# Other SBUF byte offsets for the operands of a decoder block's matmuls, seven weight forms set apart by 32 bytes, and one PSUM bank per product in the feed-forward units

## The chip, the cores and the metric

One Trainium2 chip, one core of it. The metric is device time in microseconds (us): the median of several runs, and beside it the time of one profiled execution, from which all rows of a profile come. The kernel before has a median of 838.19 us over 3 runs (837.63 to 838.41); its profiled execution took 837.62 us.

## The reference

One decoder block in float32 for one sequence of 512 tokens and a model width of 1024:

```python
h = rms_norm(x, norm_mix_pre)
proj = h @ w_in                                  # 1024 -> all q, k, v, gates
o_gla = gla_mixer(...)                           # chunked gated linear attention, 4 heads
o_nsa = nsa_mixer(...)                           # compressed, selected and window attention, 8 heads
mixed = sigmoid(merge_gla) * (o_gla @ w_proj_gla) + sigmoid(merge_nsa) * (o_nsa @ w_proj_nsa)
x = x + rms_norm(mixed @ w_out, norm_mix_post)
h = rms_norm(x, norm_ffn_pre)
f = (silu(h @ w_ffn_gate) * (h @ w_ffn_up)) @ w_ffn_down      # 1024 -> 2816 -> 1024
x = x + rms_norm(f, norm_ffn_post)
```

## The kernel before

**Products in three matmuls.** A float32 operand is split into a high part (a cast to the matmul's reduced float type, `F32R`) and a low part (the rest). A product of weights and activations is three matmuls for each block of 128 inputs: high weights with high activations, high weights with low activations, low weights with high activations (`prod`, L208 to L210, and the same three in the other product helpers). A matmul has a stationary operand, a block of 128 columns of weights, which a weight load brings into TensorE ahead of it, and a moving operand, a strip of 128 to 512 columns of activations. In a row such as `ps_mm<-hT_hi,w_d0h` the moving operand stands first and the stationary one second. Only the token-major products (L318 to L320) have it the other way: tokens stationary, weights moving.

**Seven products for eight.** Most of the input projection (`in_unit`, product at L422), of the feed-forward network (`unit`, L1588) and of its down projection (`down_product`, L1900) goes by a scheme of seven block products: the tokens fall into two halves of 256, the inputs into two halves, and sums and differences of weight blocks (forms a11, s2, s3, s1, a22, s4, a12) meet sums and differences of activation blocks (forms b11, t2, t3, t1, t4, b22, b21). So nearly all matmuls there move 256 columns, in a run of 12 per product (21 in the down projection). A weight pair of 1024 columns holds two forms: a11 and a12, s1 and s2, s3 and s4.

**Stages, in order of time.** Token-major products and the pre-norm; the input projection in 12 units; gated linear attention; sparse attention, with the rest of the input and merge projections woven in (512-column matmuls); the output projection by token halves (256 columns); three plain feed-forward blocks; 19 feed-forward units by seven products, the first two or three of them interleaved with each other; the part of the down projection that is not in the scheme (512 columns); the down projection by seven products; the last norm and the store.

**What sets the order.** The program is written as a sequence in Python; a tile framework puts in the semaphores and the places of tiles, and `tc.issue_after` pins some instructions behind others. Each engine then runs its own list in order. SyncE's queue fetches raw weights; ScalarE (ACT) casts the high parts and writes negated copies of raw weights; GpSimd (POOL) issues the transfers that add the raw weights to those, which makes low parts without VectorE; VectorE (DVE) makes the remaining low parts, the sums and differences of weights, and reads the products out of PSUM. `unit(n)` runs through its seven products in the order a11, s2, s3, s1, a22, s4, a12. After a11, ACT copies the bank piece `r1` into `us` (L1605); DVE adds the later pieces (L1592); at the end ACT applies Silu to `wk` and to `r1` (L1601).

**Where tiles lie in SBUF.** A tile's byte offset in its partition follows from the order and the sizes of the allocations in its pool. Rows of 1024 float32 are multiples of 128 bytes, so a small tile (a vector of constants, a mask) shifts all that lie behind it in a pool by the rest of its size. No line of the kernel before speaks of such offsets. Weights of the streams alternate between two buffers of `whi` and two of `wlo`; others go to `w_d0h`, `w_d0l`, `w_d1h`, `w_d1l`, `w_uu`, `w_rw`, `w_hl`, `w_g3h`, `w_g3l`, `we`, in the input projection to `s0`, `s1`, `s2` and `uu`.

**PSUM.** Eight banks of 512 float32, allocated as four names (`mm`, `acc`, `tp`, `sc`) of two buffers each. A feed-forward unit takes both buffers of one name: `r1` and `rb` share a bank, and so do `r2` and `ra`; the four names take turns over four units. A product that starts in a bank in which another piece is alive must not clear the bank (the argument `first`).

## Time and profile before

| what | value |
|---|---|
| median of 3 runs | 838.19 us (837.63 to 838.41) |
| the profiled execution | 837.62 us |
| its span, first to last instruction | 835.8 us |
| mean granted TensorE clock | 0.999 of full speed |
| TensorE busy | 829.5 us, 5676 matmuls |
| VectorE busy | 655.4 us |
| ScalarE busy | 525.8 us |
| GpSimd busy | 178.4 us |

PE stands for TensorE's matmuls and PEld for its weight loads. Matmuls are pipelined: one starts long before the one ahead of it has ended, and the ends are modelled. So the mean time of one matmul in a group is longer than the distance from its start to the next start; the difference between two groups is what counts.

### The profile page before, as it was taken

The page shows a single profiled execution, that of the slowest core. Times are in us where ns is not written, and L with a number is a line of the kernel's source. Part 1 is how long each engine was busy: PE and PEld are TensorE (multiplying, and loading weights), DVE is VectorE, ACT ScalarE, POOL GpSimd, SP SyncE. Part 2 cuts the span into 40 slices and gives each one's busy share as a digit, 9 for nine tenths or more (in the row PEclk, how much of TensorE's full clock was granted, in tenths as well). Part 3 has the DMA queues.
Part 4 walks back from the last instruction along what each step waited for, and adds up shares of the span by engine and source line. Part 5 has one row for each costly group of instructions (what it writes and reads, how often), then busy time and mean ns, then how long its engine had stood idle before and what let it go on. Part 6 is the DMA issues. An engine that isn't in the chain of part 4 may idle for free.

```text
span 835.8 us, 14964 instructions
## 1 busy us (share of the span) xinstructions
PE 829.5 (99%) x5676; PEld 763.9 (91%) x5676; DVE 655.4 (78%) x1225; ACT 525.8 (63%) x953; POOL 178.4 (21%) x217
## 2 busy tenths in 40 slices
PE   9999999999999999999999999999999999999997
PEld 8999999988888888888878998999999999889996
DVE  7877989956678988877585388998777779739985
ACT  7765687646536878877445588576555667435543
POOL 0223222422321111111001355111111110001444
PEclk9999999999999999999999999999999999999999
DMA  7588788421233444444148759488777772325222
GB/s 256 143 220 185 172 178 184 91 76 50 84 130 92 98 114 121 107 110 105 39 126 327 198 150 235 113 224 205 194 195 184 188 160 65 106 83 177 89 102 102
DMA packets 45449, 120.75 MB, mean 144 GB/s; under 512 B 5981, under 2 KB 11373, under 8 KB 45249
## 3 DMA queue, kind: packets, MB, share of 16 engines
q1 hardware_dynamic: 30720, 82.62, 29.9%
q0 software_dynamic: 14080, 36.76, 24.7%
q8 instruction: 44, 0.72, 0.3%
q10 hardware_dynamic: 576, 0.41, 0.2%
q14 instruction: 29, 0.23, 0.1%
HBM read 105.10 MB, written 4.19 MB: 131 GB/s over the span
## 4 chain that ended last, share of the span: by engine, by line
PE 94%; DVE 3%; ACT 1%; DMA 0%; issue 0%; SPq 0%; DVEq 0%; ACTq 0%
PE ps_mm L208 6%; PE ps_mm L209 6%; PE ps_mm L210 6%; PE ps_mm L1588 6%; PE ps_sc L1588 5%; PE ps_tp L1588 5%; PE ps_acc L1588 5%; PE ps_sc L1900 4%; PE ps_mm L422 4%; PE ps_tp L422 4%; PE ps_acc L422 3%; PE ps_sc L422 3%; PE ps_tp L1137 2%; PE ps_acc L1900 2%; PE ps_mm L1900 2%; PE ps_sc L210 1%
## 5 line engine op out<-in xcount | busy, mean ns | idle before, releaser
L79 ACT CAST whi<-wraw 128x1024 fp32r<-128x1024 f32 (+3 forms) x56 | 54.2, 968 | 50.9 <-issue 13.3
L208 PE MATMUL ps_mm<-hT_hi,whi 128*128 128x512 f32 x152 | 61.8, 407 | 0.0
L86 DVE TENSOR_TENSOR wlo<-wraw,whi 128x1024 fp32r<-128x1024 f32 (+3 forms) x41 | 44.8, 1093 | 20.8 <-ACT whi L79 16.8
L210 PE MATMUL ps_mm<-hT_hi,wlo 128*128 128x512 f32 x152 | 60.0, 395 | 0.0
L209 PE MATMUL ps_mm<-hT_lo,whi 128*128 128x512 f32 x152 | 59.9, 394 | 0.0
L1096 ACT ACTIVATE p<-p,mx 128x512 f32<-128x512 f32 (+1 forms) x64 | 35.8, 559 | 9.2 <-DVE mx L1094 8.4
L226 DVE TENSOR_TENSOR pl<-ps_tp,ph 128x512 fp32r<-128x512 f32 (+1 forms) x64 | 31.2, 489 | 10.2 <-ACT ph L225 9.3
L1094 DVE CUSTOM_DVE_ANT_0 p<-ps_sc,causal 128x512 f32<-128x512 f32 (+1 forms) x64 | 30.0, 485 | 7.4 <-PE ps_sc L1087 7.2
L210 PEld LDWEIGHTS ps_mm<-hT_hi,wlo 128*128 128x128 f32 x152 | 28.6, 188 | 6.4 <-DVE wlo L86 0.3
L1463 POOL DMA_DIRECT2D w_uu<-in_w_up x19 | 16.8, 882 | 81.2 <-PE ps_mm L1588 20.9
L208 PEld LDWEIGHTS ps_mm<-hT_hi,whi 128*128 128x128 f32 x152 | 28.6, 188 | 5.5
L83 POOL DMA_DIRECT2D wlo<-wraw x15 | 13.2, 879 | 94.3 <-ACT wlo L82 93.8
L209 PEld LDWEIGHTS ps_mm<-hT_lo,whi 128*128 128x128 f32 x152 | 28.7, 189 | 4.4
L225 ACT CAST ph<-ps_tp 128x512 fp32r<-128x512 f32 (+1 forms) x64 | 26.4, 414 | 4.4 <-PE ps_tp L1137 3.7
L1137 PE MATMUL ps_tp<-ident,p 128*128 128x128 f32 x160 | 27.7, 272 | 0.0
L1137 PEld LDWEIGHTS ps_tp<-ident,p 128*128 128x128 f32 x160 | 20.8, 140 | 7.1
L208 PE MATMUL ps_mm<-gla_hi,whi 128*128 128x512 f32 x64 | 26.2, 409 | 0.0
L210 PE MATMUL ps_mm<-gla_hi,wlo 128*128 128x512 f32 x64 | 25.2, 394 | 0.0
L209 PE MATMUL ps_mm<-gla_lo,whi 128*128 128x512 f32 x64 | 25.2, 393 | 0.0
L1481 ACT CAST w_d1h<-s 128x1024 fp32r<-128x1024 f32 x13 | 13.6, 1050 | 16.2 <-issue 12.8
L1481 ACT CAST w_d0h<-s 128x1024 fp32r<-128x1024 f32 x12 | 12.6, 1050 | 17.2 <-issue 12.7
L1881 POOL TENSOR_TENSOR y<-y,us 128x256 f32<-128x256 f32 x6 | 6.8, 1155 | 71.8 <-DVE us L1878 71.8
(1270 smaller groups left out, 3436.1 us busy)
## 6 DMA issues: line engine op xcount, KB each, us to landing
wraw<-in_w_t SPq DMA_DIRECT2D x28, 512.0 KB, 3.6
wraw<-in_w_gate SPq DMA_DIRECT2D x21, 512.0 KB, 4.2
rw<-in_w_up SPq DMA_DIRECT2D x19, 512.0 KB, 4.7
wlo<-wraw POOLq DMA_DIRECT2D x15, 512.0 KB, 4.5
wlo<-in_w_gate POOLq DMA_DIRECT2D x13, 512.0 KB, 7.2
urw<-in_w_t SPq DMA_DIRECT2D x12, 512.0 KB, 5.7
w_uu<-in_w_up POOLq DMA_DIRECT2D x19, 256.0 KB, 4.1
raw<-in_w_down SPq DMA_DIRECT2D x10, 448.0 KB, 3.3
```

What stands on the lines that cost most here:

```text
L79: self.cast = self.nc.scalar.copy(hi[:, :cols], raw[:, :cols])
L86: self.nc.vector.tensor_tensor(out=lo[:, :cols], in0=raw[:, :cols], in1=hi[:, :cols].bitcast(F32), op=OP.subtract)
L208: pe.matmul(ps[:, t], wh[:, c], xh(k)[:, t], start=(k == 0), stop=False)
L209: pe.matmul(ps[:, t], wh[:, c], xl(k)[:, t], start=False, stop=False)
L210: marks.append(pe.matmul(ps[:, t], wl[:, c], xh(k)[:, t], start=False, stop=(k == ktot - 1)))
L226: return dve.tensor_tensor(out=lo, in0=src, in1=hi.bitcast(F32), op=OP.subtract)
L422: pe.matmul(o, w[:, c], x_of(b, q, low), start=(first and q == 0 and i == 0), stop=(q == 3 and i == 2), skip_group_check=True)
L1094: dve.tensor_tensor_reduce(out=o, in0=s, in1=causal[:, S - n:S], scale=-1.0, scalar=-NEG, op0=OP.add, op1=OP.min, accum_out=mx[:, i:i + 1])
L1096: act.activation(out=o, in_=o, func=AF.Exp, scale=-1.0, bias=mx[:, i:i + 1], accum_out=z[:, i:i + 1])
L1137: queued["turn"] = pe.transpose(tp[:, i * 128:(i + 1) * 128], p[:, OFF[i] + k * 128:OFF[i] + (k + 1) * 128], ident)
L1588: pe.matmul(o, w[:, c], x[q], start=(first and q == 0 and i == 0), stop=(q == 3 and i == 2), skip_group_check=True)
L1900: pe.matmul(o, w[:, c], x[q], start=(first and q == 0 and i == 0), stop=(q == KH - 1 and i == 2), skip_group_check=True)
```

## The change

**One buffer for the stream weights.** Both pairs of `whi` and `wlo` become views into one tile `wbuf` of 4 x 1024 + 128 columns (class `Regions`). `regions.pair(i, shift)` gives pair 0 or 1, moved by `shift` columns; `SHIFT` is 16 columns (64 bytes), `TURN` 8 columns (32 bytes).

**Offsets.** Constants are packed into one small tile, other small tiles are moved or new (`cst`, `room`, `off2`, `off4`, the 16 spare columns of `hlc`), some allocations change their order (a `room` pass fixes the places of the feed-forward tiles), and `wbuf` is used with `SHIFT` for 256-column products and without it for 512-column ones. The byte offsets modulo 128 of the matmuls' operands become:

| operands | before | after |
|---|---|---|
| `hT_hi`, `hT_lo` (activations; reused for activation forms) | 96 | 96 |
| `t1` to `t4` forms of the input projection | 64 | 96 |
| `h2h`, `h2l`; `x4h`, `x4l`; `x` (b22) in the feed-forward part | 0 | 96 |
| `x5h`, `x5l` | 32 | 96 |
| `gla_hi`, `bh`, `bl`, attention's `q`, `ph`, `pl`, `kas` ... | 0 | 96 |
| stream weights (`whi`, `wlo`, then `wbuf`), 256 columns | 96 | 32 |
| stream weights, 512 columns | 96 | 96 |
| `s1`, `s2` | 96 | 32 |
| `s0` and `uu` of the input projection, `w_g3` | 64 | 32 |
| `w_rw`, `w_hl` | 0 | 32 |
| `w_d0`, `w_d1`, `w_uu` | 32 | 32 |
| `we` | 32 | 96 |
| down projection, high activation forms | 0, 32, 64, 96 | 96, but 32 for one of them |
| down projection, low weights, where the low activations lie at 32 | 64 or 96 | 96 |

**Seven forms set apart.** Seven pairs of weights lie 32 bytes further, at 64 in place of 32: the `a` pairs of input units 0, 5 and 6 (`slot_of`), the gate pairs of feed-forward units N0+3 and N0+9 (`prep_g`), and the down forms 0 and 6 of the sequence (`make`).

**The difference between the two operands.** Take a matmul and the one behind it on TensorE, and the byte offset of the moving operand of the first minus that of the stationary operand of the second, modulo 128. By this the matmuls of reduced float type fall into four groups. Of those with 256 columns:

| difference | before | after |
|---|---|---|
| 0 | 1153 | 115 |
| 32 | 648 | 158 |
| 64 | 951 | 3402 |
| 96 | 923 | 0 |

Of those with 512 columns nearly all but the ones in the stages of the output and the plain feed-forward blocks were at 0 and stay there; after the change 1052 are at 0, 24 at 64 and 3 at 32, and before it about 280 were at 32 or 96. The 158 at 32 are the products of the seven forms and a few at the start of the feed-forward units.

**PSUM.** From unit N0+2 on a feed-forward unit takes two names of two buffers, (`tp`, `sc`) or (`mm`, `acc`) in turn, and each of `r1`, `r2`, `rb`, `ra` has a bank of its own, so that s3 and s1 start their banks; the last unit takes `mm` and `sc`. Units N0 and N0+1 take `tp` and `sc` in the old way.

**Small things.** The mask `triu` is loaded and cast by POOL at the gates in place of DVE later; the mask `keep` is set once in place of twice; the low gate of head 3 and the factors of linear attention have other rooms; the differences of gate 3 are made one unit earlier.

On ACT, at the ends of two of the feed-forward units, before the change (`us` is the copy of the first product, `sl` holds Silu's results, `w_...` are weight parts):

```order
L1601 ACTIVATE sl<-wk 128x256
L1459 CAST whi<-wraw 128x1024
L1601 ACTIVATE sl<-ps_tp 128x256
L1461 ACTIVATE wlo<-wraw 128x1024
L1605 COPY us<-ps_sc 128x256
```

and at the same place after it:

```order
L1636 ACTIVATE sl<-wk 128x256
L1492 CAST wbuf<-wraw 128x1024
L1636 ACTIVATE sl<-ps_tp 128x256
L1494 ACTIVATE wbuf<-wraw 128x1024
L1640 COPY us<-ps_mm 128x256
```

The order is the same; the unit that starts takes the names `mm` and `acc` in place of `sc` alone.

On PE, where the third and fourth feed-forward units (banks `mm` and `acc`) begin inside the first ones, before the change:

```order
L1588 MATMUL ps_sc<-x4l,w_g3h 128x256
L1588 MATMUL ps_sc<-x4h,w_g3l 128x256
L1588 MATMUL ps_mm<-hT_hi,w_d1h 128x256
L1588 MATMUL ps_mm<-hT_lo,w_d1h 128x256
L1588 MATMUL ps_acc<-hT_hi,whi 128x256
L1588 MATMUL ps_acc<-hT_lo,whi 128x256
L1588 MATMUL ps_acc<-hT_hi,wlo 128x256
```

and where units begin inside others after it:

```order
L1623 MATMUL ps_tp<-hT_lo,wbuf 128x256
L1623 MATMUL ps_tp<-hT_hi,wbuf 128x256
L1623 MATMUL ps_mm<-hT_hi,wbuf 128x256
L1623 MATMUL ps_mm<-hT_lo,wbuf 128x256
L1623 MATMUL ps_tp<-x4h,wbuf 128x256
L1623 MATMUL ps_tp<-x4l,wbuf 128x256
L1623 MATMUL ps_sc<-hT_hi,w_hl 128x256
```

The first products of later units stand at other places among those of the first three units; from the sixth unit on the order on PE is the same as before.

The diff, cut to its core:

```diff
+SHIFT = 16
+TURN = 8
+class Regions:
+    def __init__(self, pool, first):
+        self.buf, self.turn = pool.tile([128, 4 * 1024 + 128], F32R, name="wbuf"), first
+    def pair(self, i, shift, cols=1024):
+        at = 2048 * (i % 2) + shift
+        return self.buf[:, at:at + cols], self.buf[:, at + 1024:at + 1024 + cols]
+    def next(self, shift=0):
+        self.turn += 1
+        return self.pair(self.turn - 1, shift)
...
-                hi = self.pool.tile([128, 1024], F32R, tag="whi", bufs=2, name="whi")
-                lo = self.pool.tile([128, 1024], F32R, tag="wlo", bufs=2, name="wlo")
+                hi, lo = self.regions.next(SHIFT if key in self.shifted else 0)
...
     def slot_of(j, what):
         n = 3 * j + (1 if what == "a" else 0 if what == "s1" else 2)
-        return slots[n % 5]
+        at = TURN if (j, what) in ((0, "a"), (5, "a"), (6, "a")) else 0
+        return [x[:, at:at + 1024] for x in slots[n % 5]]
...
-        slots.extend([wts.tile([128, 1024], F32R, tag="w" + x, bufs=2, name="w" + x) for x in ("hi", "lo")]
-                     for _ in range(2))
+        slots.extend((regions.pair(0, SHIFT), regions.pair(1, SHIFT, 1024 + TURN)))
...
-h2h, h2l = quads("h2h", 4, F32R, "hh"), quads("h2l", 4, F32R, "hl")
+h2h, h2l = quads("h2h", 4, F32R, "hh"), quads("h2l", 2, F32R, "hl")
+h2l23 = hlc(F32R, "h2l23")[:, 0:2048].rearrange("p (b a t) -> p b a t", b=2, a=2)
...
     def prep_g(n, after=None):
-        hi, lo = w_slot(("w", "g3", "w")[(n - N0) % 3])
+        hi, lo = w_slot(("w", "g3", "w")[(n - N0) % 3], SHIFT + (TURN if n in (N0 + 3, N0 + 9) else 0))
...
     def unit(n, between=None):
-        tag = ("mm", "acc", "tp", "sc")[(n - N0 + 2) % 4]
-        p1, p2 = bank(tag), bank(tag)
-        r1, rb, r2, ra = p1[:, 0:256], p1[:, 256:512], p2[:, 0:256], p2[:, 256:512]
+        if n < N0 + 2:
+            p1, p2 = [bank(("tp", "sc")[n - N0]) for _ in range(2)]
+            r1, rb, r2, ra = p1[:, 0:256], p1[:, 256:512], p2[:, 0:256], p2[:, 256:512]
+        else:
+            tags = ("mm", "sc") if n == KF - 1 else (("tp", "sc"), ("mm", "acc"))[(n - N0) % 2]
+            r1, r2, rb, ra = [bank(tag)[:, 0:256] for tag in tags for _ in range(2)]
...
-        product(rb, "s3", "t3", False)
+        product(rb, "s3", "t3", n >= N0 + 2)
...
-        product(ra, "s1", "t1", False)
+        product(ra, "s1", "t1", n >= N0 + 2)
...
-        lambda: dform("t3", [quad(x, F32R, "dt3" + x) for x in ("d0h", "d0l", "e0", "e1")], left, h1),
+        lambda: dform("t3", [quad(x, F32R, "dt3" + x) for x in ("e0", "e1", "d0h", "d0l")], left, h1),
...
+    FAR = ("b11", "t2", "t3", "t1")
...
-        hi, lo = [x[:, :KW] for x in w_slot(("w", "g3", "w")[j % 3])]
+        which = ("w", "g3", "w")[j % 3]
+        at = (SHIFT if which == "w" else 0) + (TURN if j in (0, 6) else 0)
+        hi, lo = [x[:, c:c + KW] for x, c in zip(w_slot(which, 0), (at, at + (SHIFT if b in FAR else 0)))]
```

102 lines of the change are left out of this document (58 added, 44 removed).

## The prediction

> **What bounds the kernel now.** I read the page first: the span, the busy times, the chain of work that ended last.
>
> ```profile
> span 835.8 us, 14964 instructions
> PE 829.5 (99%) x5676; PEld 763.9 (91%) x5676; DVE 655.4 (78%) x1225; ACT 525.8 (63%) x953; POOL 178.4 (21%) x217
> PE 94%; DVE 3%; ACT 1%; DMA 0%; issue 0%; SPq 0%; DVEq 0%; ACTq 0%
> ```
>
> PE is busy for 829.5 of 835.8 us. Then the waits of PE alone (line, what it waited for; us in total, times, longest):
>
> ```profile
> PE ps_acc L149 <- DVE eps L136: 0.9, 1, 0.9
> PE ps_sc L1588 <- ACT us L1605: 0.5, 1, 0.5
> PE ps_mm L1588 <- DVE w_hl L1488: 0.4, 1, 0.4
> ```
>
> All waits come to 1.8 us, so only fewer matmuls or a shorter distance between their starts can move the end by more. The change issues the same matmuls. So the question is the distance, and I went from the page to single matmuls. The timeline (start, duration, engine, line, tiles) at both ends of some runs:
>
> ```profile
> 457.60 0.28 PE L208 MATMUL ps_sc<-hT_hi,w_uu 128*128 128x256 f32 x1
> 468.37 0.28 PE L210 MATMUL ps_acc<-hT_hi,we 128*128 128x256 f32 x1
> ...
> 582.78 0.28 PE L1588 MATMUL ps_mm<-hT_hi,whi 128*128 128x256 f32 x1
> 583.50 0.28 PE L1588 MATMUL ps_mm<-hT_hi,w_d0h 128*128 128x256 f32 x1
> 587.62 0.28 PE L1588 MATMUL ps_mm<-hT_hi,w_d0l 128*128 128x256 f32 x1
> ```
>
> From 457.60 to 468.37 lie 95 matmuls of 256 columns: 113.4 ns from start to start. From 582.78 to 583.50 lie 6: 120 ns. From 583.50 to 587.62 lie 35: 117.7 ns. The granted clock is full in all three (the windows below), so it isn't the clock. Groups kept apart by shape show the same by their mean (last number but one, ns), which is the distance and some 163 ns of pipeline:
>
> ```profile
> L208 PE MATMUL ps_mm<-hT_hi,w_d1h 128*128 128x256 f32 x8 | 2.2, 276 | 0.0
> ...
> L209 PE MATMUL ps_mm<-hT_lo,w_d1h 128*128 128x256 f32 x8 | 2.2, 281 | 0.0
> ...
> L1588 PE MATMUL ps_mm<-hT_hi,w_d0h 128*128 128x256 f32 x8 | 2.2, 281 | 0.0
> ...
> L422 PE MATMUL ps_sc<-hT_lo,whi 128*128 128x256 f32 x4 | 1.1, 283 | 0.0
> ...
> L422 PE MATMUL ps_acc<-t2l,s1h 128*128 128x256 f32 x4 | 1.1, 283 | 0.0
> L422 PE MATMUL ps_acc<-t2h,s1h 128*128 128x256 f32 x4 | 1.1, 281 | 0.0
> L422 PE MATMUL ps_acc<-t2h,s1l 128*128 128x256 f32 x4 | 1.1, 279 | 0.0
> ...
> L1395 PE MATMUL ps_sc<-h2h,whi 128*128 128x256 f32 x12 | 3.4, 286 | 0.0
> L1396 PE MATMUL ps_sc<-h2l,whi 128*128 128x256 f32 x12 | 3.3, 279 | 0.0
> ...
> L208 PE MATMUL ps_tp<-hT_hi,whi 128*128 128x512 f32 x32 | 12.4, 389 | 0.0
> ...
> L208 PE MATMUL ps_acc<-h2h,we 128*128 128x512 f32 x8 | 3.2, 396 | 0.0
> ```
>
> The windows are 457.6 to 468.3, 478.3 to 483.6, 583.4 to 587.7, 111.4 to 115, 95 to 98.7, 498.8 to 502.8, 715 to 754 and 511.9 to 520.4. Line, engine and size don't order these rows; the byte offsets of the two operands do, by the difference that the change's second table counts. `hT_hi` (96) with `whi` (96) is difference 0: 283, always 120 ns once it runs. `t2` (64) with `s1` (96) is 96, `h2h` (0) with `whi` (96) is 32: uneven, 118 and 117 to 118 ns on average. `hT_hi` (96) with `w_d1h`, `w_d0h` or `w_uu` (32) is 64: 276 in one place and 281 in two others, for the same tiles. With 512 columns difference 0 takes 389 and 96 takes 396.
>
> So difference 64 has **two rhythms**, 113.4 and 117.7 ns. Inside a run neither changes to the other: the 96 matmuls from 457.60 stay fast, the 46 from 478.2 and the 37 from 583.4 stay slow. What stands ahead of a run seems to choose. After a settled run of difference 0 it is slow in all of 9 cases, of which the first and the last:
>
> ```profile
> L1588 PE MATMUL ps_sc<-hT_hi,w_d1h 128*128 128x256 f32 x4 | 1.1, 281 | 0.0
> ...
> L1588 PE MATMUL ps_mm<-hT_hi,w_d0h 128*128 128x256 f32 x7 | 2.0, 281 | 0.0
> ```
>
> After difference 96 it is either. After fp32 matmuls or a stall it was fast three times and slow once (478.2). After difference 32 it was fast in 4 of 5 cases; the first of those four and the fifth, which follows one single such matmul:
>
> ```profile
> L1588 PE MATMUL ps_tp<-hT_lo,w_d0h 128*128 128x256 f32 x4 | 1.1, 276 | 0.0
> ...
> L1900 PE MATMUL ps_sc<-dt1e,wlo 128*128 128x256 f32 x6 | 1.7, 280 | 0.0
> ```
>
> **The change part by part.** *The long runs.* The change puts 3402 of 3675 matmuls at difference 64, in runs of up to 756, and each of the seven forms set apart is two runs of 11 or 12 (in the down projection one of 20) at difference 32 ahead of a long one. By the cases above such a run starts fast, and I take 113.4 for it. The stages today, by line and window (window, its length, PE busy and matmuls, PEld the same, clock, DMA share, GB/s; the last row is of all instructions, with DVE third, ACT fourth and POOL fifth):
>
> ```profile
> 42.00:167.00 125.00, 120.73 (x1008) 120.33 (x1008) 1.00 0.75 172
> ...
> 554.00:712.00 158.00, 157.03 (x1333) 156.75 (x1332) 1.00 0.71 170
> ...
> 754.00:826.00 72.00, 70.34 (x588) 69.78 (x588) 1.00 0.33 112
> ...
> 520.00:554.00 34.00, 32.96 (x269) 31.96 (x268) 33.45 (x56) 21.65 (x34) 4.23 (x5) 1.00 0.66 160
> ```
>
> Input projection (first row): 120.73 us for 1008, 119.8 ns each; 0.9 of that is what breaks by other matmuls add, which stay, so 118.8. After: 935 at 113.4 and 69 at 117.3, 113.7 on average. Gain 1004 x 5.1 ns = 5.1 us. Feed-forward units (second row): 117.8, without breaks 117.7; after 1289 at 113.4 and 37 at 117 to 120, 113.6. Gain 1326 x 4.1 = 5.4 us. Down projection (third row): 119.6, without the breaks at the norm 118.1; after 543 at 113.4 and 41 at 117.5, 113.7. Gain 584 x 4.3 = 2.5 us.
>
> *Other stages.* Output projection: its present runs are already half at 113.4; 48 go to difference 0 (`w_d1l` to `we`) at 120, and what follows them will be slow: +0.2 us, between 0 and +0.5. Plain blocks: 170 at 64 in place of 0 and 32, cut up by fp32 sums: -0.5, between 0 and -0.7. Attention and plain blocks with 512 columns: some 280 move from 32 or 96 to mostly 0, worth up to 7 ns each (396 against 389), but where attention waits for softmax nothing: -0.7, between 0 and -1.9. Start of the feed-forward units (last row): DVE is busy 33.45 of 34 us, so faster matmuls wait for DVE there; the interleaving moves later products to other places. I take -0.2, between +1.0 (a product that comes before its weights) and -2.0 (PE's whole lost time there, 34 less 269 matmuls at some 118 ns).
>
> *Four banks.* A unit's s3 no longer shares a bank with r1. No wait of PE stood on that, so nothing is gained. The price could be the earlier reuse, two units on in place of four. ACT and PE at the end of one unit:
>
> ```profile
> 621.55 0.41 ACT L1601 ACTIVATE sl<-wk 128x256 f32<-128x256 f32 x1
> 621.95 1.06 ACT L1459 CAST whi<-wraw 128x1024 fp32r<-128x1024 f32 x1
> 622.90 0.38 ACT L1601 ACTIVATE sl<-ps_sc 128x256 f32<-128x256 f32 x1
> ...
> 621.75 0.28 PE L1588 MATMUL ps_sc<-x4h,wlo 128*128 128x256 f32 x1
> 621.86 0.28 PE L1588 MATMUL ps_mm<-hT_hi,w_g3h 128*128 128x256 f32 x1
> ```
>
> The last reader of the bank, Silu, ends at 623.28, 1.4 us into the next unit; the unit that takes the bank again starts a whole unit (some 9.6 us) later. That covers it by 8 us. Only N0+2 takes `sc` straight from N0+1; there s3 comes two products (2.7 us) in, so at worst some 0.5 us once, which the +1.0 above holds. *The rest* (one `triu` cast on POOL in place of DVE, `keep` once, gate 3 one unit earlier) is 0: POOL is at 21%, and DVE loses work.
>
> *Cover.* As PE takes 4% less, the others must follow. All instructions of the three stages (PE, PEld, DVE, ACT, POOL):
>
> ```profile
> 42.00:167.00 125.00, 125.00 (x1037) 124.11 (x1036) 108.60 (x181) 86.25 (x145) 37.31 (x47) 1.00 0.75 172
> ...
> 554.00:711.00 157.00, 157.00 (x1334) 156.93 (x1334) 127.03 (x227) 100.51 (x157) 24.30 (x29) 1.00 0.72 171
> ...
> 754.00:826.00 72.00, 72.00 (x610) 71.84 (x608) 61.69 (x78) 36.02 (x53) 25.89 (x22) 1.00 0.33 112
> ```
>
> The fullest is DVE in the input projection, 108.6 of 125 us, and after it 108.6 of some 120. It still fits; but each of the 12 units shortens by 0.43 us, and where DVE reads a product late now, a matmul that overwrites that bank may bind by some tenths: +0.2 us, which I leave at 0, up to +1.0.
>
> The sum: -5.1 -5.4 -2.5 +0.2 -0.5 -0.7 -0.2 = -14.2 us. The profiled execution took 837.62 us, the median is 0.57 above it: 823.4 profiled, **824.0** as a median.
>
> One rule bears on the floor. The Trainium skill, TensorE: Matmul & The Clock Gate, section "Back-to-back issue gap", gives an isolated gap of columns / 2.4 + 2.5 ns, 109.2 for 256. If fast runs went by it, the sum would be 14 us lower, an estimate from that page, 810; no row here is under 276, so I keep 113.4.
>
> **Rivals.** *Half of the long runs are slow.* A stall or the fp32 matmuls between input units may reset the rhythm, and the rule after difference 32 rests on 5 cases. Each long run is worth 4.3 ns a matmul; half of the 2767 in the three stages is 5.9 us: 829.9. For it: 478.2 and the one case of five. Against: the runs in question follow 11 or more matmuls at 32, not one.
>
> *All are slow.* Then input -1.0, units +0.2, down -0.2, output +0.6, plain blocks and the start 0, 512 columns -0.7: -1.1, 837.1. For it: 478.2 to 483.6 are output runs of just this kind. Against: 96 in a row at 276.
>
> *Offsets do nothing*, and the rows differ for another reason that goes with place and not with address: 838. The Trainium skill speaks for it: SBUF — State Buffer, section "SBUF: two separate sides", says that PE's side never waits on anyone, and TensorE: Matmul & The Clock Gate, "Step-by-step: what each phase is for", that loading weights takes no read bandwidth from the running matmul. Against: `whi` at 283 and `w_d0h` at 281 follow each other in one window with the same activations, and 389 against 396 has no other difference.
>
> *Slower: VectorE pays for the offsets.* Tiles go from 0 to 32 and 96; if DVE's work took 20% longer for it, the input projection would take DVE's 130 us (+5), the start of the units 40 (+6), the units 152 (-5), the down projection 74 (+2), the rest -1: 845. It decides from 10%, where DVE's 108.6 us fill the new input stage. Against it, a low part into `w_hl` at 0 and one into `w_d0l` at 32:
>
> ```profile
> 611.75 1.23 DVE L1488 TENSOR_TENSOR w_hl<-s,w_hl 128x1024 fp32r<-128x1024 f32 x1
> ...
> 619.59 1.22 DVE L1488 TENSOR_TENSOR w_d0l<-s,w_d0h 128x1024 fp32r<-128x1024 f32 x1
> ```
>
> **How the numbers follow.** Forecast 0.64, half 0.20, all slow 0.08, offsets nothing 0.03, slower 0.05. A measurement of this kernel tells 0.2% (1.7 us) from no change. Faster: 0.64 + 0.20 and a little of all slow, 0.85; same 0.10; slower 0.05. The forecast's own ends come from the bounds above: 512 columns 1.2 us more, start of the units 1.8, plain blocks and output 0.4 make 820.6, and the losses 0.3 + 0.2 + 0.7 + 1.2 + 1.0 make 827.4. The range goes from 820.5 up to 832.5, past the half case; it leaves out all slow, nothing and slower, 0.16.
>
> **What would show it.** Right: in the profile after, L422's, L1588's and L1900's groups of 256 columns at 276 to 277, 281 only in short runs; the windows of the three stages at 113 to 114 ns a matmul; PE's waits still under 3 us. The seven forms show as groups near 279 to 281 with 276 behind them. Half: some units at 281 throughout, from one form set apart to the next. Wrong: 281 everywhere; or PE waits of many us on DVE or on ACT's Silu; or DVE's 1.22 us grown.

## The result, and the profile after

The change takes **829.69 us** (median of 4 runs, 829.38 to 829.88) against 838.3 us of the kernel before (4 runs, 837.63 to 838.72): a ratio of 0.990, 95% interval 0.988 to 0.9915. The forecast was 824.0 us with a range of 820.5 to 832.5. The sign and the range held; 5.7 us of the 14.2 that were forecast did not come. The range held because it had been drawn past the rival "half of the long runs are slow"; the sum itself missed.

The page of the changed kernel, its first lines and its chain of waits:

```profile
span 827.6 us, 14964 instructions
PE 819.2 (99%) x5676; PEld 754.1 (91%) x5676; DVE 652.3 (79%) x1223; ACT 524.6 (63%) x953; POOL 178.3 (22%) x216
PE 92%; DVE 3%; DMA 1%; issue 1%; ACT 1%; POOL 1%; SPq 0%; DVEq 0%; POOLq 0%; ACTq 0%
```

PE is as full as before and issues the same 5676 instructions; the span fell by 8.2 us because the starts moved closer together. The waits of PE alone (line, what it waited for; us in total, times, longest), the four longest, of which the first stood there before; all come to 3.8 us, against 1.8 before:

```profile
PE ps_acc L162 <- DVE consts L150: 0.9, 1, 0.9
PE ps_mm L1623 <- DVE w_d0l L1521: 0.8, 1, 0.8
PE ps_mm L338 <- ACT hT_hi L278: 0.7, 1, 0.7
PE ps_mm L443 <- DVE us L447: 0.4, 1, 0.4
```

The three long stages by line and window (window, its length, PE busy and matmuls, PEld the same, clock, DMA share, GB/s). Line 443 is the input projection, 1623 the feed-forward units, 1938 the down projection (422, 1588 and 1900 before):

```profile
42.00:160.00 118.00, 115.72 (x1002) 115.24 (x1003) 1.00 0.79 179
...
554.00:700.00 146.00, 145.84 (x1282) 145.50 (x1280) 1.00 0.75 181
...
750.00:808.00 58.00, 58.00 (x496) 58.00 (x496) 1.00 0.40 132
```

That is 115.5, 113.8 and 116.9 ns a matmul, where the forecast had 113.7, 113.6 and 113.7. (A row counts a matmul that only reaches over the window's edge; from start to start the last one is 117.5.) The groups by shape say where the rest lies. In the units, from 583.4 to 587.7 us (the window that stood at 281 before), all are at 276 ns:

```profile
L1623 PE MATMUL ps_sc<-x5h,w_uu 128*128 128x256 f32 x8 | 1.5, 276 | 0.0
L1623 PE MATMUL ps_sc<-hT_lo,w_d0h 128*128 128x256 f32 x2 | 0.6, 276 | 0.0
```

In the input projection they are so too, but from 88.2 to 103 us, behind a wait for VectorE, they are not:

```profile
L443 PE MATMUL ps_tp<-t4h,uu 128*128 128x256 f32 x8 | 1.6, 281 | 0.0
L443 PE MATMUL ps_acc<-t2h,s1h 128*128 128x256 f32 x4 | 1.1, 281 | 0.0
```

And the down projection, here from 764.5 to 773 us, has neither of the two rhythms; its means go from 281 to 283:

```profile
L1938 PE MATMUL ps_mm<-dt2h,wbuf 128*128 128x256 f32 x14 | 2.7, 282 | 0.0
L1938 PE MATMUL ps_mm<-dt3e,wbuf 128*128 128x256 f32 x14 | 2.6, 281 | 0.0
L1938 PE MATMUL ps_mm<-dt1e,w_g3h 128*128 128x256 f32 x5 | 1.4, 283 | 0.0
```

By stage, from first start to first start in the two profiled executions, after less before: input projection -3.71 us, units -4.74, down projection -0.52, the stages with 512 columns -0.67, plain blocks -0.18, start of the feed-forward part +0.06, output projection +0.61, the start of the program +0.70, its end +0.22; together -8.2.

### The profile page after: what moved, and what is told of

The parts are those of the page before. It is cut to its first block, busy times and chain, and to the rows that moved or that the text cites. A ratio compares the mean times of both kernels' runs of the same rounds, so it can differ in the third digit from the quotient of the medians.

```text
span 827.6 us, 14964 instructions
## 1 busy us (share of the span) xinstructions
PE 819.2 (99%) x5676; PEld 754.1 (91%) x5676; DVE 652.3 (79%) x1223; ACT 524.6 (63%) x953; POOL 178.3 (22%) x216
## 4 chain that ended last, share of the span: by engine, by line
PE 92%; DVE 3%; DMA 1%; issue 1%; ACT 1%; POOL 1%; SPq 0%; DVEq 0%; POOLq 0%; ACTq 0%
PE ps_mm L224 6%; PE ps_mm L225 6%; PE ps_mm L226 6%; PE ps_sc L1623 6%; PE ps_acc L1623 5%; PE ps_tp L1623 5%; PE ps_sc L1938 4%; PE ps_mm L443 4%; PE ps_tp L443 4%; PE ps_mm L1623 4%; PE ps_sc L443 3%; PE ps_acc L443 3%; PE ps_tp L1154 2%; PE ps_mm L1938 2%; PE ps_acc L1938 2%; PE ps_acc L224 1%
## 5 line engine op out<-in xcount | busy, mean ns | idle before, releaser
L96 ACT CAST wbuf<-wraw 128x1024 fp32r<-128x1024 f32 (+3 forms) x56 | 54.2, 968 | 46.6 <-issue 13.3
L103 DVE TENSOR_TENSOR wbuf<-wraw,wbuf 128x1024 fp32r<-128x1024 f32 (+3 forms) x41 | 44.4, 1083 | 22.4 <-ACT wbuf L96 18.3
L224 PE MATMUL ps_mm<-hT_hi,wbuf 128*128 128x512 f32 x152 | 61.8, 407 | 0.0
L225 PE MATMUL ps_mm<-hT_lo,wbuf 128*128 128x512 f32 x152 | 60.0, 395 | 0.0
L226 PE MATMUL ps_mm<-hT_hi,wbuf 128*128 128x512 f32 x152 | 59.8, 393 | 0.0
L226 PEld LDWEIGHTS ps_mm<-hT_hi,wbuf 128*128 128x128 f32 x152 | 28.5, 188 | 6.5 <-DVE wbuf L103 0.4
L224 PEld LDWEIGHTS ps_mm<-hT_hi,wbuf 128*128 128x128 f32 x152 | 28.6, 188 | 5.5
L100 POOL DMA_DIRECT2D wbuf<-wraw x15 | 13.0, 870 | 94.5 <-ACT wbuf L99 94.5
L225 PEld LDWEIGHTS ps_mm<-hT_lo,wbuf 128*128 128x128 f32 x152 | 28.7, 189 | 4.5
L224 PE MATMUL ps_mm<-gla_hi,wbuf 128*128 128x512 f32 x64 | 26.0, 407 | 0.0
L225 PE MATMUL ps_mm<-gla_lo,wbuf 128*128 128x512 f32 x64 | 25.2, 393 | 0.0
L226 PE MATMUL ps_mm<-gla_hi,wbuf 128*128 128x512 f32 x64 | 25.1, 393 | 0.0
L1514 ACT CAST w_hl<-s 128x1024 fp32r<-128x1024 f32 x11 | 11.6, 1051 | 18.7 <-issue 12.2
```

The costliest lines, as they stand in the source:

```text
L96: self.cast = self.nc.scalar.copy(hi[:, :cols], raw[:, :cols])
L103: self.nc.vector.tensor_tensor(out=lo[:, :cols], in0=raw[:, :cols], in1=hi[:, :cols].bitcast(F32), op=OP.subtract)
L224: pe.matmul(ps[:, t], wh[:, c], xh(k)[:, t], start=(k == 0), stop=False)
L225: pe.matmul(ps[:, t], wh[:, c], xl(k)[:, t], start=False, stop=False)
L226: marks.append(pe.matmul(ps[:, t], wl[:, c], xh(k)[:, t], start=False, stop=(k == ktot - 1)))
```

## The experiments

"Fast" and "slow" below are the two rhythms, 113.3 and 117.8 ns from start to start, and "uneven" is a distance that changes from matmul to matmul. Behind every probe stands the same question: what chooses between them?

**1. The rhythms by themselves.** A kernel of matmuls on zeros, which computes nothing of the block: runs of 256 columns with the activations at 96 and the weights' offset varied.

```
def run(d, n):                      # n matmuls at difference d (modulo 128)
    for _ in range(n):
        mm(96, (96 - d) % 128)      # activations' and weights' offset
...
for d in (16, 32, 48, 64, 80, 96, 112):
    run(0, 48)
    run(d, 96)
```

> This kernel computes nothing of the block: it runs some 6950 matmuls of 256 columns on zeros, with chosen byte offsets of both operands, and nothing else works beside them. Theory (the prediction's): the distance between starts follows the offset of the moving operand less that of the NEXT stationary one: 120 ns at 0, 117 to 118 uneven at 32 and 96, and 113.4 or 117.7 at 64; behind a steady run of 0 a run at 64 is slow (117.7), behind 1 to 24 matmuls at 32 that follow a run of 0 it is fast (113.4). Pairs that keep 64 to the next weights but 0 to their own run at 113.4 or 117.7, pairs the other way at 120. The triples of the down projection (activations at 96 and 32, weights at 32 and 96), all at 64, run like any other run at 64. Rival: the distance goes with place, time and other engines' work; then with nothing else working all segments have one distance, or their order doesn't follow the offsets.

Measured: difference 64 ran at 113.33 or at 117.78 ns and never changed inside a run, of which the longest had 448 and 248 matmuls; the others lay between 116.7 and 120.0. The run of 96 at 64, and the same difference with the operands' offsets exchanged (activations at 32, weights at 96), both without any other engine at work:

```profile
68.60:78.30 9.70, 9.70 (x88) 9.70 (x87) 1.00 0.01 2
187.00:197.80 10.80, 10.80 (x94) 10.80 (x93) 1.00 0.00 0
```

A matmul lasts 0.28 us and counts where any part of it lies in the window: (9.70 + 0.28) / 88 is 113.4 ns, (10.80 + 0.28) / 94 is 117.9. The down projection's own order (activations at 96 and 32 in turn, weights at 32 and 96, difference 64 throughout, modulo 128) was uneven at 117.8 and never fast. So the two rhythms are real and need nothing else on the chip; but behind difference 0 the runs here were fast, where the kernel before had them slow 9 times in 9. That contradiction stood until experiment 7. (Counted modulo 256, as from there on, the two rows above are at 192 and at 64, the "0" of this probe is 128, and the down projection's order here goes 192, 64, 192, so that its difference was not constant after all.)

**2. With traffic.** The same with VectorE, ScalarE and SP's DMA busy all the time.

```
-    pass
+    background(460)    # DVE adds, ACT scales, SP loads 512 KB tiles
```

> The same matmuls, with DVE adding and ACT copying 1024 columns all the time and SyncE fetching weights into two rooms. Theory: the same distance in every segment within 0.5 ns, and the same choice of rhythm behind each entry. Rival (other engines' traffic sets the rhythm): some segments at 64 change their rhythm against the quiet kernel, or change in the middle of a run of 400.

Measured, the same two windows, now with DVE (third), ACT (fourth) and 250 GB/s:

```profile
68.60:78.30 9.70, 9.70 (x88) 9.70 (x87) 9.45 (x8) 9.45 (x9) 0.00 (x0) 1.00 0.80 258
187.00:197.80 10.80, 10.80 (x94) 10.80 (x93) 10.49 (x10) 10.48 (x11) 0.00 (x0) 1.00 0.84 251
```

Every distance agrees within 0.03 ns, and so does the choice of every run that has no wait ahead of it. Traffic neither makes nor chooses the rhythm; the order of matmuls ahead does, and behind a wait for VectorE it went either way.

**3. The seven forms not set apart.**

```
-        at = TURN if (j, what) in ((0, "a"), (5, "a"), (6, "a")) else 0
+        at = 0
...
-        hi, lo = w_slot(("w", "g3", "w")[(n - N0) % 3], SHIFT + (TURN if n in (N0 + 3, N0 + 9) else 0))
+        hi, lo = w_slot(("w", "g3", "w")[(n - N0) % 3], SHIFT)
...
-        at = (SHIFT if which == "w" else 0) + (TURN if j in (0, 6) else 0)
+        at = SHIFT if which == "w" else 0
```

> The change without the seven forms set apart: those weights lie at 32 like the others, all other offsets as in the change. Theory of the prediction (the forms choose the rhythm of the run behind them): long runs in the input projection and in the feed-forward units fall into 117.7 ns for want of them; half of 2250 matmuls by 4.3 ns is 4.8 us: 834.5 (832 to 838). Rival (waits of PE choose the rhythm, the forms don't): within 1.5 us of the change's 829.7, with the slow runs behind other waits.

Measured: 829.71 us (828.14 to 830.4), ratio to before 0.9894 (0.9879 to 0.9908): the same as the change. By stage the profiled execution lost 2.7 us in the input projection, since its runs of 335 and 442 matmuls went slow; the units ran 1091 matmuls fast without any form set apart (-0.25 us); the first stage and the start of the feed-forward part were 1.7 us shorter, which is as much as they vary between kernels that are alike there. The input projection's row, which stood at 115.72 for 1002 in the change:

```profile
42.00:160.00 118.00, 116.54 (x984) 116.11 (x985) 1.00 0.78 177
```

So in this execution the forms set apart are worth 2.7 us in the input projection and nothing in the units and the down projection; the medians don't show that gain, since the other stages made up for it.

**4. The change with the old banks.**

```
-        if n < N0 + 2:
-            p1, p2 = [bank(("tp", "sc")[n - N0]) for _ in range(2)]
-            r1, rb, r2, ra = p1[:, 0:256], p1[:, 256:512], p2[:, 0:256], p2[:, 256:512]
-        else:
-            tags = ("mm", "sc") if n == KF - 1 else (("tp", "sc"), ("mm", "acc"))[(n - N0) % 2]
-            r1, r2, rb, ra = [bank(tag)[:, 0:256] for tag in tags for _ in range(2)]
+        tag = ("mm", "acc", "tp", "sc")[(n - N0 + 2) % 4]
+        p1, p2 = bank(tag), bank(tag)
+        r1, rb, r2, ra = p1[:, 0:256], p1[:, 256:512], p2[:, 0:256], p2[:, 256:512]
```

> The change with the feed-forward units' PSUM as before (r1 with rb and r2 with ra in one bank, four names in turn over four units). Theory: the four banks gave nothing and cost nothing but the order of the first units; 829.7 within 1.0 us. Rival: PE's waits at the start of the feed-forward units (some 2.5 us in the changed kernel's profile between 517 and 550 us) come from the new interleaving of units; then 1 to 2.5 us faster, 827.2 to 828.7.

Measured: 833.93 us (833.01 to 834.4), 4.24 above the change. 1202 of 1258 matmuls of the units are slow. The timeline shows how a run falls (start, duration, engine, line, tiles), first ScalarE's copy of r1, then PE from the last matmul of s2 on:

```profile
620.75 0.36 ACT L1638 COPY us<-ps_mm 128x256 f32<-128x256 f32 x1
```

```profile
621.11 0.28 PE L1621 MATMUL ps_mm<-hT_hi,w_hl 128*128 128x256 f32 x1
621.22 0.33 PE L1621 MATMUL ps_mm<-hT_hi,w_d0h 128*128 128x256 f32 x1
621.39 0.28 PE L1621 MATMUL ps_mm<-hT_lo,w_d0h 128*128 128x256 f32 x1
621.50 0.28 PE L1621 MATMUL ps_mm<-hT_hi,w_d0l 128*128 128x256 f32 x1
621.62 0.28 PE L1621 MATMUL ps_mm<-hT_hi,w_d0h 128*128 128x256 f32 x1
621.74 0.28 PE L1621 MATMUL ps_mm<-hT_lo,w_d0h 128*128 128x256 f32 x1
```

Up to 621.22 the matmuls start 113 ns apart. The copy ends at 621.11, when s3, which goes into the bank that it read, should start within 0.1 us; its first matmul takes 0.33 us in place of 0.28 and the next comes 170 ns later, and from there the distance is 118. In the kernel before s3 starts 24 x 117.7 = 2.82 us into a unit and in a fast one 2.72, while the copy waits in ScalarE's queue behind a weight copy of 1.05 us (L1494) and comes no earlier: that 0.1 us is what the slow pace had spared it.

ScalarE's copy is one case of it; VectorE's reads of a shared bank do the same. The run ahead had fallen at 612.78 us, where s1 goes into the bank whose other half VectorE has just read (first VectorE, then PE):

```profile
612.26 0.42 DVE L1625 TENSOR_TENSOR us<-ps_sc,us 128x256 f32<-128x256 f32 x1
```

```profile
612.78 0.34 PE L1621 MATMUL ps_sc<-hT_hi,w_d0h 128*128 128x256 f32 x1
```

The next start comes 175 ns later. The first fall, at 557.87 us, comes 0.06 us after another such read (it ends at 557.81), so all three of this execution are of this kind.

**5. The four banks alone**, in the kernel before, with the lines of experiment 4 the other way round (`-` and `+` exchanged).

> The kernel before with one part of the change alone: the feed-forward units' four results in PSUM banks as the change has them, all offsets as before. Theory (the shared bank costs only once matmuls are fast, since at 117.7 ns the third product starts after the copy of the first has ended): the same as before, 838.3 within 1 us. Rival (the four banks remove a wait that is there at any pace, and the 4.2 us between the change and the change with the old banks are theirs alone): some 834, 4 us faster.

Measured: 837.96 us (836.42 to 839.04, 10 runs), ratio 0.9993 (0.9984 to 1.0002). Nothing. So the shared bank costs something only in fast units, and neither part of the change has the units' 4.7 us without the other.

**6. The down projection at one offset (modulo 128).**

```
-            hi, lo = [at[4 * j + i].rearrange(...)[:, 0:m, :] for j in range(2)]
+            ...    # low parts 16 columns on in their tiles: activations at 96, high and low
...
-        hi, lo = [x[:, c:c + KW] for x, c in zip(w_slot(which, 0), (at, at + (SHIFT if b in FAR else 0)))]
+        hi, lo = [x[:, c:c + KW] for x, c in zip(w_slot(which, 0), (at, at))]
```

> The change with the down projection's four forms b11, t2, t3, t1 laid out so that high and low parts of the activations both lie at 96 and both parts of the weights at 32 (in the change the activations alternate between 96 and 32 and the weights between 32 and 96, difference 64 throughout). Theory (difference 64 gives a fast rhythm only where the offset itself stays the same from matmul to matmul): those 336 matmuls run at one of the two steady rhythms instead of unevenly at 118.5 ns; 1.7 us less than the change (828.0) where they are fast, 0.2 us less (829.5) where they are slow. Rival (the unevenness has another cause, such as VectorE's additions into the result banks or the loads): still uneven at 118.5, 829.7.

Measured: 830.76 us (830.26 to 831.16), ratio 0.9909 (0.9892 to 0.9926). The forms are as uneven as in the change (768 to 775 us):

```profile
L1958 PE MATMUL ps_mm<-dt2h,wbuf 128*128 128x256 f32 x15 | 2.6, 280 | 0.0
L1958 PE MATMUL ps_mm<-dt2l,wbuf 128*128 128x256 f32 x6 | 1.7, 282 | 0.0
L1958 PE MATMUL ps_mm<-dt3d0h,wbuf 128*128 128x256 f32 x3 | 0.8, 283 | 0.0
```

My theory failed as stated. The addresses gave the reason: the high parts lie at 224 modulo 256 and the low parts at 96, so that the differences go 192, 64, 192. (Against the change it lost 1.6 us on a run of 370 matmuls in the units, which went slow behind a wait at 564 us and in the change went fast.)

**7. What stands ahead, again, with the real triples.** Matmuls on zeros, nothing of the block: high x high, high x low, low x high, and runs of 36 at difference 64 behind 12 or 24 at each other one.

```
for n in (12, 24):
    for x in (0, 16, 32, 48, 80, 96, 112):
        run(0, 48); run(64, 36); run(x, n); run(64, 36); run(x, n); run(64, 36)
```

> This kernel computes nothing of the block: only matmuls on zeros in the order of the real products (high part with high, high with low, low with high), all activations at 96, the weights' offset varied, nothing else working. Each piece is a run of 36 at difference 64 between 12 or 24 matmuls at one other difference. Theory (what the distance of starts is when the run begins chooses its rhythm): every 64-run stays at one of 113.3 or 117.8 ns from its second matmul to its last; behind the steady 120 ns of difference 0 or 112 it is always the same of the two, and behind the uneven differences (80, 96) it depends on the count. At least one difference gives the fast rhythm behind both 12 and 24 and from both rhythms; my guess is 0 or 32. Rival (chance, or the memory of something longer than the run ahead): the same piece gives different rhythms at its two places, and no difference is reliable. The down projection's triples with activations at 96 and 32 alternating: 117.7 uneven both times, and what follows either.

Measured: behind 0, 32 and 96 always fast, behind 16 and 112 always slow, behind 48 and 80 either. That agreed neither with the kernel before nor with experiment 1. Sorted again with offsets modulo 256, the three agree: behind 0 a run at 192 had been slow 28 times in 28 (the kernels) and a run at 64 fast 19 times in 19 (this probe); behind 128 a run at 192 had been fast 26 times in 28 (experiments 1 and 2). (The down projection's triples were uneven again, 116.7 ns.)

**8. Offsets modulo 256, put to the test.** Again matmuls on zeros and nothing of the block; the activations at 224, weights at 224 less the difference, all modulo 256.

```
for d in (192, 64):
    for x in (0, 128, 160, 32, 96, 224):
        for n in (12, 24, 48):
            run(x, n); run(d, 36)
# then one operand's low part 256, 128 or 64 bytes further on
for low, wlow in ((256, None), (128, None), (64, None), (None, 288), (None, 160), (None, 96)):
    run(128, 24); run(192, 48, low, wlow); run(192, 36)
    run(0, 24);   run(192, 48, low, wlow); run(192, 36)
```

> This kernel computes nothing of the block: matmuls on zeros in the order of the real products, nothing else working. The runs so far, sorted again with offsets counted modulo 256 and not 128, say: the change's difference 64 is really 192 (activations at 224, weights at 32); 0 has always been followed by the slow rhythm of 192 and by the fast one of 64, 128 nearly always by the fast one of 192, 160 by either. Theory (the period is 256 bytes, and what stands ahead decides): behind 12, 24 and 48 matmuls at 0 the 36 at 192 run at 117.8 ns and the 36 at 64 at 113.3; behind 128 the other way round; behind 160 and 32 mixed. With the low activations 256 bytes further on 192 stays as steady as without; with them 128 or 64 further it is uneven, and the same for the weights' low parts. Rival (the period is 128, and what looked like a rule is chance): 0 and 128 behave alike, 64 and 192 too, and a low part 128 further on changes nothing.

Measured, as groups (tiles; count; busy, mean ns). Behind 0 the run at 192 (weights `wa`, `la`) is slow and the run at 64 (`wb`, `lb`) fast; behind 128 the other way round:

```profile
L83 PE MATMUL ps_one<-m_high,wa 128*128 128x256 f32 x12 | 3.4, 281 | 0.0
...
L83 PE MATMUL ps_one<-m_high,wb 128*128 128x256 f32 x12 | 3.3, 276 | 0.0
...
L83 PE MATMUL ps_one<-m_low,wa 128*128 128x256 f32 x11 | 3.0, 276 | 0.0
...
L83 PE MATMUL ps_one<-m_low,wb 128*128 128x256 f32 x12 | 3.4, 280 | 0.0
```

The windows are 34.2 to 38.1 us, 167.8 to 171.6, 56.9 to 60.4 and 190.4 to 194.3. All 12 runs at 192 behind 0 and 128 that began without a wait, and all 9 at 64, went as said. Difference 160 was followed by a fast stretch at 192 three times and by a slow one once, where 512 columns stood ahead of it. With the low activations 256 bytes on nothing changed; 128 or 64 on, uneven; the weights' low parts 64 on, uneven too. The period is 256 bytes. One answer I had not expected: with the **weights' low parts 128 bytes on** (differences 192, 192, 64 in turn) the run became fast within six matmuls, behind 128 and also behind 0, and stayed fast afterwards. (With the low activations 128 bytes on, which is uneven, the differences are 192, 64, 192: the same cycle. So the difference alone doesn't set the pace where an operand's offset changes from matmul to matmul.) Window 499.5 to 504 us, behind 24 at difference 0:

```profile
L83 PE MATMUL ps_one<-m_high,lb 128*128 128x256 f32 x14 | 3.9, 276 | 0.0
L83 PE MATMUL ps_one<-m_high,wa 128*128 128x256 f32 x14 | 3.9, 276 | 0.0
```

**9. The seven forms at 128 in place of 160.**

```
-TURN = 8
+TURN = 16
```

> The change with its seven forms set apart by 64 bytes in place of 32: their difference is 128 modulo 256 in place of 160. Theory (128 is followed by the fast rhythm, 160 by either): every run at 192 behind a set-apart form of 11 or more matmuls is fast, in the input projection, the units and at the down projection's first three products; the one slow run behind such a form in the change (88 matmuls of the input projection, 0.4 us) goes, and since runs that begin behind a stall stay a toss, 829.3, between 828.0 and 830.5. Rival (the form's offset is of no account): some of these runs are slow, as with 160.

Measured: 830.43 us (830.2 to 830.77). Of the eight runs behind such a form of 11 or 12 matmuls, outside the down projection, seven were fast, as with 160 in the change; the one slow, at 93 us, is the same as there. My theory that 128 is reliable where 160 is not has no support in the kernel, whatever the probe did; what is different at 93 us stays open. Two long runs behind waits, at 138 and at 564 us, went slow that were fast in the change, 2.2 us.

**10. The down projection at one offset modulo 256.** As experiment 6, with the low parts 240 columns on in place of 16.

```
-            h, l0, l1 = [... (cols[-2], SHIFT), (cols[-1], SHIFT))]
+            h, l0, l1 = [... (cols[-2], LOW), (cols[-1], LOW))]      # LOW = 240
```

> The change with the down projection's four forms laid out as in the run before last on it, but with the low activations 960 bytes on in place of 64, so that high and low lie at 224 modulo 256 (there: 224 and 96), weights at 32. Theory (the offset must stay the same modulo 256): these 336 matmuls run at one steady rhythm; fast 1.7 us less than the change (some 828.0), slow 0.2 us less (829.5); which of the two the form of 20 matmuls ahead at 160 leaves open. Rival (the unevenness belongs to the low parts' place in other tiles): uneven as there, 118 to 119 ns, 829.7.

Measured: 829.34 us (827.74 to 832.68, the widest spread of all), ratio 0.9896 (0.987 to 0.9923). The same groups as in experiment 6, in the same window:

```profile
L1958 PE MATMUL ps_mm<-dt2h,wbuf 128*128 128x256 f32 x15 | 2.5, 276 | 0.0
L1958 PE MATMUL ps_mm<-dt2l,wbuf 128*128 128x256 f32 x6 | 1.7, 276 | 0.0
L1958 PE MATMUL ps_mm<-dt3d0h,wbuf 128*128 128x256 f32 x3 | 0.8, 276 | 0.0
```

No form but the one set apart is uneven any more: 16 products went steady, fast from 765 to 795 us and slow ahead of that and behind a wait at 795. In this execution the down projection gained 0.7 us and the stages with the slow stretches behind the waits at 138 and 564 us lost 2.3. This is the plain picture of what is left: a wait tosses the rhythm, and the run behind it keeps the result for up to 370 matmuls, 1.6 us.

**11. The mix that pulls fast.** From experiment 8: no form set apart, the weights' low parts in the shared buffer at 160 and their high parts at 32, the down projection as in experiment 10.

```
-        at = 2048 * (i % 2) + shift
-        return self.buf[:, at:at + cols], self.buf[:, at + 1024:at + 1024 + cols]
+        at = 2112 * (i % 2) + shift
+        lo = at + 1024 + (32 if shift else 0)
+        return self.buf[:, at:at + cols], self.buf[:, lo:lo + cols]
...
-TURN = 8
+TURN = 0
```

> The change with three edits: no form is set apart any more; the weights' low parts in the shared weight buffer (a third of the input projection's products, some of the units', two thirds of the down projection's) lie at 160 modulo 256 and their high parts at 32, so that the differences go 192, 192, 64 in these products; the down projection's activations at 224 as in the run before. In the probe this mix ran at 113.3 ns both behind the slow and behind the fast rhythm and left it fast. Theory (the mix pulls the slow rhythm into the fast one, and a run at 192 keeps it until a stall): input projection, units and down projection fast but for the stretch from a stall to the next such product; against the change -0.8 in the input projection (the slow stretch and the forms set apart), -0.3 in the units, -1.9 in the down projection, output and start as they are: 826.7, between 825.5 and 828, and its runs closer together than the run before's (827.7 to 832.7). Rival (two cases of a probe were luck): long slow runs behind the stalls stay as they were, 829 to 831.

Measured: **826.97 us** (826.1 to 828.01), ratio to before 0.9862 (0.9846 to 0.9878). The first unit of the input projection began slow, and the first product with its weights in the shared buffer ended that. PE around 52.9 us:

```profile
52.63 0.28 PE L444 MATMUL ps_sc<-hT_lo,s 128*128 128x256 f32 x1
52.75 0.28 PE L444 MATMUL ps_sc<-hT_hi,s 128*128 128x256 f32 x1
52.87 0.28 PE L444 MATMUL ps_acc<-hT_hi,wbuf 128*128 128x256 f32 x1
52.99 0.28 PE L444 MATMUL ps_acc<-hT_lo,wbuf 128*128 128x256 f32 x1
53.11 0.40 PE L444 MATMUL ps_acc<-hT_hi,wbuf 128*128 128x256 f32 x2
...
53.69 0.28 PE L444 MATMUL ps_acc<-hT_lo,wbuf 128*128 128x256 f32 x1
53.81 0.39 PE L444 MATMUL ps_acc<-hT_hi,wbuf 128*128 128x256 f32 x2
54.03 0.28 PE L444 MATMUL ps_acc<-hT_lo,wbuf 128*128 128x256 f32 x1
54.15 0.28 PE L444 MATMUL ps_acc<-hT_hi,wbuf 128*128 128x256 f32 x1
54.26 0.28 PE L444 MATMUL ps_acc<-t2h,wbuf 128*128 128x256 f32 x1
```

The first starts lie 118 ns apart, those from 53.69 on 113 (the rows round to 10 ns; x2 stands for two matmuls). All five products of this kind that began slow ended fast. The units ran 1090 matmuls in one piece fast, and in the down projection 551 of 588 were fast (143 in the change).

**12. The same in four more places**: the input projection's other slots and the buffers of the output projection's first form.

```
-    sform0 = [room[:, c:c + 1024 + TURN] for c in (0, 1024)]
+    sform0 = [room[:, c:c + 1024] for c in (0, 1024 + 32)]
...
+            if (i, x) != (2, "l"):
+                s2.tile([128, 32], F32, name="gap%d%s" % (i, x))
...
+    for _ in range(2):
+        ffn.tile([128, 1056], F32R, tag="rw", bufs=2, name="room")
```

> The run before with the same shift of the weights' low parts in four more places: the three other slots of the input projection's weight sums, and the two buffers that hold the third output column's weights, the first of the output projection's runs of 256 columns. Theory (such a product pulls the slow rhythm into the fast one): the slow stretches that the run before still had from 43 to 53 us and from 92.6 to 102.5 (84 matmuls each) and the first 96 and the 48 behind difference 0 of the output projection (from 451) go fast, each matmul 4.4 ns: -0.37 -0.37 -0.64 = -1.4 against 826.97, so 825.6, between 824.6 and 826.6. Rival (which rhythm comes is set when the stretch begins, and these products do not change it): the same stretches stay slow somewhere, 827.

Measured: **826.1 us** (825.38 to 826.54), ratio to before 0.9851 (0.9834 to 0.9867); 3.6 us below the change, with no run of one near a run of the other. The forecast of 825.6 was 0.5 too good. The first unit of the input projection, window 42.9 to 52.7 us in experiment 11 and 42.4 to 52 here:

```profile
L444 PE MATMUL ps_sc<-t2h,s1h 128*128 128x256 f32 x4 | 1.1, 281 | 0.0
```

```profile
L444 PE MATMUL ps_sc<-t2h,s1h 128*128 128x256 f32 x4 | 1.1, 276 | 0.0
```

All three stretches named beforehand went fast (-0.37, -0.33 and -0.61 us). Six more products of the mix began slow or at the steady 120 ns of difference 0, and all six ended fast: 11 of 11 over both kernels. This is the best kernel of the study; its page begins:

```profile
span 824.8 us, 14972 instructions
PE 816.5 (99%) x5676; PEld 750.5 (91%) x5676; DVE 652.1 (79%) x1227; ACT 525.1 (64%) x953; POOL 182.0 (22%) x216
```

## Why the prediction was right and wrong, by its steps

*What bounds the kernel: right.* What moved the end is the distance between starts. The same 5676 instructions of PE take 8.2 us less of span, and experiments 1 and 2 show both rhythms without any other work and unchanged under full traffic.

*"The byte offsets of the two operands do" (order the rows): right, with the wrong period.* I counted modulo 128. The period is 256 (experiments 6, 8 and 10), so the change's "64" is 192 and its forms set apart are at 160. And a constant difference is not enough, each operand's own offset has to stay: in the change's down projection the difference is 192 modulo 256 throughout, with activations at 224 and 32 and weights at 32 and 96 in turn, and it is uneven (281 to 283); with both offsets constant it is steady (experiment 10).

*"Such a run starts fast", behind a form set apart: right 7 times in 8, but worth less than I took.* It carried 2.7 us, all of it in the input projection (experiment 3, one execution). In the units the run behind the wait at 564 us is fast or slow by itself, and I had no such wait in the sum.

*Input projection, -5.1 forecast, -3.71 measured.* The distance was met where it was fast. Missing are 139 matmuls at that difference that were not fast, 0.5 us, and the gaps longer than 135 ns, which grew from 0.31 to 1.23 us together. The longest is a wait for VectorE's `us`, of the kind that the prediction named and left at 0 ("up to +1.0"); the run behind it went slow.

```profile
87.11 0.28 PE L443 MATMUL ps_mm<-t1h,s2l 128*128 128x256 f32 x1
87.80 0.39 PE L443 MATMUL ps_mm<-t4h,uu 128*128 128x256 f32 x1 [0.41 <-DVE us L447]
```

*Units, -5.4 forecast, -4.74 measured: right in size, wrong in cause.* The step that failed is the one on the **four banks: "No wait of PE stood on that, so nothing is gained."** No wait stood on it in the profile of before because the matmuls were slow. At the fast distance it binds, and in experiment 4 each of the three times it did so the run fell back to slow. Without the four banks the units gain 0.25 us in place of 4.74 (experiment 4: 5.54 us above 113.3 ns for each matmul, before 5.79, in the change 1.06), and the four banks alone gain nothing (experiment 5). What I looked for was the price of an edit in the kernel as it was; its worth lay in the kernel that the other edits made.

*Down projection, -2.5 forecast, -0.52 measured: wrong.* I counted 543 matmuls at difference 64 as one kind. 336 of them alternate between two offsets in both operands and had no steady rhythm (the 281 to 283 above; experiments 1 and 6 are uneven with other mixtures). With one offset modulo 256 they do, and with the mix the stage gains another 1.5 us against the change.

*Output projection, +0.2 forecast, +0.61 measured.* Mechanism right: the runs behind the steady 120 ns of `we` are slow. But the first 95, behind 512 columns, were slow as well, which I had costed only in the rival "all are slow" (+0.6). *Plain blocks* -0.18 for -0.5, *512 columns* -0.67 for -0.7, *start of the feed-forward part* +0.06 for -0.2: inside their bounds. The program's start, +0.70, was not in the sum; it goes with the wait for `hT_hi` at line 338 above, and it varies by itself: the input projection began at 42.46 and 42.43 us in experiments 9 and 12 and at 43.07 and 43.06 here and in 6, at 42.37 in the kernel before and at 43.02 in experiment 5, which changes nothing there.

Together 1.39 + 0.66 + 1.98 + 0.41 + 0.32 + 0.03 + 0.26 + 0.70 + 0.22 = 6.0 us of span less than forecast.

*The signs.* Of those named for "right", the 276 in the units and in most of the input projection came; the down projection's did not, and PE's waits came to 3.8 us in place of under 3. (The upper end of the forecast's own bounds took 0.2 us for the plain blocks where 0 to -0.7 leaves 0.5: 827.7 in place of 827.4. Nothing hangs on it.)

*The rivals.* "Half of the long runs are slow" gave 829.9, and the time is 829.7; but that is luck, by the matmuls it is not that case: in the three stages 2130 of 2847 are fast, and what is missing are the waits, the runs behind them and the alternating forms. "VectorE pays for the offsets" is excluded: DVE's busy time went from 655.4 to 652.3 us. "Offsets do nothing" is excluded by experiment 1 alone. The Trainium skill, SBUF — State Buffer, "SBUF: two separate sides", which says that PE's side never waits on anyone, may hold for other engines' traffic, with which experiment 2 agrees (0.03 ns); the distance of PE's own starts does depend on where its two operands lie, 113.3 against up to 120.0 ns. The 109.2 ns that "Back-to-back issue gap" of the Trainium skill, TensorE: Matmul & The Clock Gate, gives for 256 columns appeared in no run: the lowest steady distance was 113.3.

What stays open: why the two rhythms exist at all, what a wait leaves behind that makes the next run fast or slow, and why the run at 93 us is slow behind 160 and 128 alike.

## What to carry to other kernels

An edit that costs nothing and gains nothing in today's profile can be what the next edit needs: where a change makes a stage faster, look for the waits that have only just enough slack at the old pace, and price them at the new one. When a duration has two values with nothing between, vary the layout in a probe of that one instruction before building on a rule from five cases, and let the period of the addresses be one of the unknowns. And prefer a layout that returns to the good state by itself over one that has to start in it: each wait is a new toss.

## What the runs showed of the chip that was not expected

For fp32r matmuls of 256 columns with 128 x 128 weights, at full clock, as long as each operand keeps its offset the distance of starts depends on the offset of the running activations less that of the next weights, modulo 256 bytes: 120.0 ns steady at 0, 118.7 uneven at 128, 113.3 or 117.8 steady at 64 and 192, 116.5 to 120 uneven or steady at the others that were tried. At 64 and 192 a run keeps its rhythm for as long as nothing interrupts it (448 matmuls in a probe, 1090 in a kernel), whatever DMA, VectorE and ScalarE do. Difference 0 ahead makes 192 slow and 64 fast, 128 ahead the reverse, in all 21 cases of experiment 8 (26 of 28 for 128 and 192 in experiments 1 and 2). Low weights 128 bytes from the high ones (192, 192, 64 in turn) turned a slow stretch fast, within six matmuls in the probe and within ten in the kernels, 11 times in 11 there; low activations 128 bytes from the high ones, with the same cycle of differences, made it uneven instead. With 512 columns difference 0 is the best, 226.7 ns once settled against 230 to 236 at 192. And where a matmul started a product in a PSUM bank some 0.1 us after the end of ScalarE's or VectorE's read of the other half of that bank, the next start came 165 to 222 ns later in place of 113, three times in experiment 4, and the run behind it was slow: 731 matmuls after the last of them.
